# A two-layer hybrid trunk (gated linear attention beside chunked attention) in float32: softmax's negated maximum from one pass, a head's normaliser as one power, small sums off GpSimd, heads turned later, last chunks bank by bank

## The chip, the cores and the metric

The kernel runs on one core of one Trainium2 chip. A core has five engines that work side by side: TensorE (PE, matrix products, with its weight loads as PEld), VectorE (DVE), ScalarE (ACT), GpSimd (POOL) and SyncE (SP), which here only issues transfers. The metric is the device time of one execution in microseconds (us); lower is better. Each engine takes its instructions in the order in which they were placed in its stream and waits on semaphores for the others.

## The reference

Two layers, each on x of 512 tokens by 2048 features:

```python
h = rmsnorm(x, g_pre)
z = h @ w_in                                   # 7184 columns, split into nine parts
gq, gk, gv, gg, ga, aq, ak, av, ag = split_columns(z)
log_a = log_sigmoid(ga @ w_alpha + b_alpha) / GLA_TAU
o_gla = gla_chunk_causal(gq, gk, gv, log_a)     # 4 heads, state carried over 8 chunks of 64
o_gla = rmsnorm(o_gla, g_gla) * silu(gg)        # norm within a head
o_att = chunk_band_attention(aq, ak, av, rel_bias)   # 8 heads of 128
o_att = rmsnorm(o_att, g_att) * silu(ag)
y = concatenate([o_gla, o_att]) @ w_out
return x + rmsnorm(y, g_post)
```

In attention the scores are `q k^T * 128**-0.5 + bias`, a query sees all keys of its own and of earlier chunks, the softmax runs over the keys, and each head's output is divided by its root mean square (with EPS = 1e-6 under the root) before the gate.

## The kernel before

**Products in split precision.** Every float32 operand is split into a high and a low part (`wh` and `wl` for weights, made by ScalarE at L183 and VectorE at L187), and each product is three matrix products: high by high, high by low, low by high. The weights lie in 18 blocks of 512 columns per layer, and each block in eight chunks of 256 rows. A chunk of a block, or a Strassen-like sum of chunks of two blocks, is a *job*: `load` fetches it, `high` and `low` split it, `ahead()` prepares the next jobs. `std_gemm` does one block for up to four groups of 128 tokens, chunk by chunk (24 matrix products of 512 columns a chunk over four groups); `fast_gemm` does a pair of blocks in seven sums of products (P1, P5, P6, P3, P7, P2, P4), four jobs each, 28 jobs in all, 12 products of 512 columns or 24 of 256 a job. When a sum is complete, `consume` reads the accumulators: P3 and P7 give the two halves of the pair's second block, P2 and P4 those of its first.

**Order of the blocks in a layer.** AG0 and AG1 (gate of attention, `std_gemm`), then the pairs GG, AV, QK01 with QK23, QK45 with QK67, GK with GQ, GV0 with GV1 (`PAIRS`, `fast_gemm`), then the output projection: its first two blocks by `std_gemm` (NB_IN and NB_IN + 1), its last two as one pair with `end=True`.

**Side work.** All that is not a large product is written as generators in the list `tasks`. After each job, or each group of products of a chunk, `Pace` calls `pump(n)`, which takes n steps of the first task in the list, n being `rate` per call on average. `until(cond)` takes steps without any product between them until a condition holds; `drain()` empties the list. The side work is: `attend` for a pair of heads, in the step order of `ORDER` (S scores, T transposes of the probabilities, P the product with the values, G the gate, R the turn of the head's output into the layout of the output projection; 0 to 3 are groups of 128 tokens; "-" is an empty step); `forget_gate_decay`; `transpose_q`; and `gla_heads` for two GLA heads in four units of 256 tokens each (`new`, `states`, `read`, `norm`, `gate`, `turn`).

**Who waits for whom in the program.** Heads are taken in the order 2 and 3, 0 and 1, 6 and 7, 4 and 5. `heads_done` is set at the end of `attend`. The consumer of the fourth Q and K set waits for heads 2 and 3 (L829); the forget gate, put at the head of the list, for heads 0 and 1 (L847); the first consumed half of GK/GQ for heads 6 and 7 (L866), the first of GV for heads 4 and 5 (L1034). `operand_out` (L1048) waits until a GLA head's turned output is in `og`; the chunks of the output projection come in the order `OO`, with GLA heads 0 and 1 last.

**Buffers.** Four PSUM banks `mm` hold the accumulators, four `ax` everything else. Temporaries `t` rotate through eight buffers; the gate tile `sg` that a head (L751) or a GLA unit (L912) fetches has two, the bias tile two, small statistics `sm` six. `wh` has four buffers, `wl` three.

**The planner.** The kernel is written in a framework that places the semaphores and sets each engine's order with a planner (L1191): it runs through the program with its own estimates of costs and gives an engine, whenever it is free by these estimates, the first instruction of the program that is ready by them. A step's place in the program is so a priority, not a fixed place; what the planner has put in order stays so on the chip, however long things take there.

**The steps that the change touches.** Scores: L723 adds the bias to the scores in PSUM and gives the maximum; L727 negates it on GpSimd; L728 takes exp with that as bias and the row sum as second output; after the last group L731 and L732 invert the sums and scale them, and L733 asks for a later head's bias (L698, with a fill of one corner at L699). L762 squares the output, scaled by the inverted sum; `gate` (L764) makes the head's coefficient: EPS is added on GpSimd (L399), the power -0.5 taken there (L395), the result multiplied by the inverted sum (L767), and L770 gates the four groups. L781 turns the head on TensorE, L784 scales it, L787 and L793 store it. For GLA: L904 outer products, L922 and L924 states, L937 read, L947 squares, L399 and L395 the norm, L955 the gate, L965 the turn, L976 its scaling, L105 and L106 the split, L980 the store. Output projection: L1069 and L1070 empty a bank.

## Time and profile before

| | |
|---|---|
| median of three runs | 1717.86 us (1715.18 to 1718.84) |
| the profiled execution: its own time | 1714.22 us |
| its span from first to last instruction | 1712.5 us |
| TensorE busy | 1651.8 us, 96% of the span |
| VectorE, ScalarE, GpSimd busy | 1206.1, 870.3, 207.9 us |
| mean granted TensorE clock | 0.987 |

Times in views of the trace count from the first instruction of the profiled execution. A matrix product's row gives a modelled duration that overlaps its neighbours; how fast products follow each other is seen from their starts. "[2.8 <-DVE sg L770]" behind a row says that the engine was idle for 2.8 us before it and that the instruction at L770, VectorE's write of `sg`, released it. In the list of waits a row gives the us in total, how often, and the longest. "PEclk" is the clock that the chip granted TensorE, as a share of full speed.

### The profile page before, as it was taken

To read this page: it belongs to the slowest core of one execution; us is meant where nothing else is said; L and a number is where in the kernel's file an instruction comes from. 1 tells how busy PE (TensorE), PEld (TensorE's weight loads), DVE (VectorE), ACT (ScalarE), POOL (GpSimd) and SP (SyncE) were. 2 spreads that over 40 slices of the span, in tenths; PEclk is the share of its full clock that TensorE was granted. 3 is DMA by queue.
4 is the path that set the end of the run, shared out by engine and by line. 5 is a ranking of instruction groups with operands and counts; after the bars stand their busy time and mean duration, and the time that the engine had idled before them with its cause. 6 is when DMAs were issued, how large, how long until landed. Compare 5 with 4: busy or idle time off the path is not lost.

```text
span 1712.5 us, 25057 instructions
## 1 busy us (share of the span) xinstructions
PE 1651.8 (96%) x9090; PEld 1410.9 (82%) x9090; DVE 1206.1 (70%) x1547; ACT 870.3 (51%) x1444; POOL 207.9 (12%) x368
## 2 busy tenths in 40 slices
PE   7999999999999999899989999999999999998996
PEld 5888889999987877688778878799999878776784
DVE  5746867776866875468987567767778667753787
ACT  8634544465664644335694345445556555433443
POOL 0110000011201101210212000000111112012101
PEclk9999999999999999999999999999999999999998
DMA  7986886868857787489769687868686777865994
GB/s 254 361 308 236 324 289 237 290 194 284 299 172 262 241 330 247 164 308 326 263 228 386 222 304 282 303 226 284 209 305 235 235 239 245 315 218 178 348 331 145
DMA packets 143004, 455.05 MB, mean 266 GB/s; under 512 B 15444, under 2 KB 32212, under 8 KB 142880
## 3 DMA queue, kind: packets, MB, share of 16 engines
q1 hardware_dynamic: 119984, 373.76, 63.7%
q0 software_dynamic: 22176, 78.41, 11.9%
q8 instruction: 72, 1.18, 0.3%
q10 hardware_dynamic: 720, 1.28, 0.2%
q14 instruction: 52, 0.43, 0.1%
HBM read 381.28 MB, written 72.11 MB: 265 GB/s over the span
## 4 chain that ended last, share of the span: by engine, by line
PE 87%; DMA 4%; DVE 4%; issue 2%; ACT 2%; POOL 0%; SPq 0%; DVEq 0%; POOLq 0%; ACTq 0%
PE mm L349 41%; PE mm L339 18%; PE mm L275 18%; PE ax L756 2%; DMA raw<-in_w_dram 2%; DVE wl L187 1%; PE ax L904 1%; DMA sa<-S 1%; PE ax L739 1%; PE ax L937 1%; PE ax L597 1%; ACT wh L183 1%; PE ax L720 1%; PE ax L718 1%; PE ax L719 1%
## 5 line engine op out<-in xcount | busy, mean ns | idle before, releaser
L349 PE MATMUL mm<-wh,sa 128*128 128x512 f32 x1536 | 488.1, 393 | 2.8 <-DMA sa<-S 1.6
L183 ACT CAST wh<-raw 128x1024 fp32r<-128x1024 f32 x248 | 261.9, 1056 | 293.5 <-PE mm L349 96.9
L187 DVE TENSOR_TENSOR wl<-raw,wh 128x1024 fp32r<-128x1024 f32 x248 | 301.2, 1217 | 81.7 <-PE mm L275 26.3
L183 ACT CAST wh<-H 128x1024 fp32r<-128x1024 f32 x224 | 234.6, 1051 | 210.3 <-PE mm L349 112.4
L349 PEld LDWEIGHTS mm<-wh,sa 128*128 128x128 f32 x1536 | 288.1, 188 | 64.3 <-DMA sa<-S 2.5
L187 DVE TENSOR_TENSOR wl<-H,wh 128x1024 fp32r<-128x1024 f32 x224 | 272.6, 1221 | 93.2 <-PE mm L349 26.9
L349 PE MATMUL mm<-wl,sa 128*128 128x512 f32 x768 | 301.8, 393 | 7.6 <-DVE wl L187 7.5
L339 PE MATMUL mm<-sa,wh 128*128 128x256 f32 x1280 | 236.0, 285 | 0.0
L339 PEld LDWEIGHTS mm<-sa,wh 128*128 128x128 f32 x1280 | 200.2, 191 | 0.2
L349 PE MATMUL mm<-wh,a 128*128 128x512 f32 x576 | 186.3, 397 | 2.4 <-DVE g L1070 1.4
L275 PE MATMUL mm<-wh,a 128*128 128x512 f32 x512 | 171.3, 399 | 15.1 <-ACT a L105 7.8
L339 PE MATMUL mm<-sa,wl 128*128 128x256 f32 x640 | 182.1, 285 | 0.4 <-DVE wl L187 0.4
L349 PEld LDWEIGHTS mm<-wl,sa 128*128 128x128 f32 x768 | 144.5, 188 | 41.8 <-DVE wl L187 12.1
L176 DVE TENSOR_TENSOR H<-H,raw 128x1024 f32<-128x1024 f32 x112 | 136.5, 1219 | 2.0
L349 PEld LDWEIGHTS mm<-wh,a 128*128 128x128 f32 x576 | 109.8, 191 | 26.6 <-DVE g L1070 1.9
L275 PEld LDWEIGHTS mm<-wh,a 128*128 128x128 f32 x512 | 96.9, 190 | 38.9 <-ACT a L105 9.2
L180 DVE TENSOR_TENSOR raw<-H,raw 128x1024 f32<-128x1024 f32 x48 | 58.8, 1225 | 91.4 <-DMA raw<-in_w_dram 91.4
L339 PEld LDWEIGHTS mm<-sa,wl 128*128 128x128 f32 x640 | 122.5, 191 | 0.6 <-DVE wl L187 0.6
L349 PE MATMUL mm<-wl,a 128*128 128x512 f32 x288 | 114.4, 397 | 0.3 <-DVE wl L187 0.3
L275 PE MATMUL mm<-wl,a 128*128 128x512 f32 x256 | 102.4, 400 | 0.0
L727 POOL TENSOR_SCALAR sm<-sm 128x1 f32<-128x1 f32 x64 | 34.1, 533 | 521.7 <-DVE sm L723 520.9
L339 PE MATMUL mm<-a,wh 128*128 128x256 f32 x512 | 95.2, 286 | 0.0
(191 smaller groups left out, 2418.0 us busy)
## 6 DMA issues: line engine op xcount, KB each, us to landing
raw<-in_w_dram SPq DMA_DIRECT2D x312, 512.0 KB, 4.9
sa<-S SPq DMA_DIRECT2D x192, 512.0 KB, 4.7
H<-in_w_dram SPq DMA_DIRECT2D x56, 512.0 KB, 4.7
sa<-A SPq DMA_DIRECT2D x48, 512.0 KB, 5.8
S<-g POOLq DMA_DIRECT2D x32, 512.0 KB, 7.7
oS<-g POOLq DMA_DIRECT2D x32, 512.0 KB, 6.8
sa<-oS SPq DMA_DIRECT2D x32, 512.0 KB, 5.0
sg<-t POOLq DMA_DIRECT2D x32, 256.0 KB, 5.7
```

The costliest lines, as they stand in the source:

```text
L176: nc.vector.tensor_tensor(out=h, in0=h, in1=r, op=ALU.add)
L180: nc.vector.tensor_tensor(out=r, in0=h, in1=r, op=ALU.subtract)
L183: last_cast[0] = nc.scalar.copy(self.wh, src).ins
L187: nc.vector.tensor_tensor(out=self.wl, in0=self.src, in1=self.wh.bitcast(F32), op=ALU.subtract)
L275: nc.tensor.matmul(pss[o], a[:, part, t], rhs[:, kk, :], start=(i == 0 and kk == 0 and m == 0), stop=(i == n - 1 and kk == 1 and m == 2),)
L339: nc.tensor.matmul(dst, lhs[:, kk, f], a[:, part, tok], start=(fresh and kk == 0 and m == 0 and ft % 2 == 0), stop=(c == 3 and kk == 1 and ...
L349: nc.tensor.matmul(out_ps[t], a[:, part, tok], rhs[:, kk, :], start=(fresh and kk == 0 and m == 0), stop=(c == 3 and kk == 1 and m == 2), ...
L597: nc.tensor.matmul(ps[0:96, half * 256 : (half + 1) * 256], wga[kt // 10][:, kt % 10, :], op[:, i, (kt % 2) * 256 : (kt % 2 + 1) * 256], s ...
L718: nc.tensor.matmul(ps[:, :n], self.qh[:, t], self.kh[:, :n], start=True, stop=False)
L719: nc.tensor.matmul(ps[:, :n], self.qh[:, t], self.kl[:, :n], start=False, stop=False)
L727: nc.gpsimd.tensor_scalar(out=nmx, in0=mx, scalar1=-1.0, scalar2=None, op0=ALU.mult)
L756: nc.tensor.matmul(o, self.pt[i][:, j * P : (j + 1) * P], av[hd // 4, j // 2][:, j % 2, (hd % 4) * P : (hd % 4 + 1) * P], start=(j == 0), ...
```

## The change

It has six parts.

1. **Softmax.** The scaled queries are split with -128**-0.5, so the scores come out negated, and the bias tile is negated by a ScalarE copy after its transfer, before VectorE's fill. L723 adds and takes a *minimum*, which is the negated maximum; exp runs with scale -1 and that minimum as its bias. The GpSimd negation goes.
2. **A head's normaliser.** The square is scaled by a constant, not by the inverted sum. Instead of the inverted sums a tile `el` = EPS times the squared sums is made; the coefficient is (mean square + `el`) to the power -0.5: one addition on VectorE and one power on GpSimd.
3. **Small sums.** `rms_scale`, which GLA's norm uses, adds EPS on VectorE.
4. **Turns.** A list `delayed` holds turns with a count of pumped steps: a head's turn runs eight steps after its gate, a GLA unit's five steps after its gate. `heads_done` is set by the turn of the pair's second head. `ORDER` loses its two turns and its leading and trailing pauses and gets one pause before each gate; the first pair starts after five empty steps. `pump` counts a step also when only delayed turns are left. The forget gate and `gla_heads` get more empty steps, and the rates change: 2.1 for the last four pairs, 1.7 for the first output block.
5. **GLA's gate tile** lies in `sg` for odd units and in a buffer of the bias tile for even ones.
6. **Last chunks bank by bank.** AG1 and the second output block run with lag 2, the first output block with lag 1: the last `lag` chunks are done bank after bank, and each bank is emptied when it is complete.

```diff
--- before.py
+++ after.py
@@ -116,8 +116,8 @@
     ident = cst[:, 0:P]
     chunk_ind = cst[:, 2 * P : 2 * P + 2]
     ones = cst[:, 2 * P + 2 : 3 * P + 2]
+    mhalf = cpool.tile([P, 4], F32, tag="mhalf", name="mhalf")
     later = cpool.tile([P, P], F32R, tag="later", name="later")
-    mhalf = cpool.tile([P, 4], F32, tag="mhalf", name="mhalf")
 
     CO = (0, 4, 1, 5, 2, 6, 3, 7)
     OO = (5, 4, 7, 6, 2, 3, 0, 1)
@@ -225,22 +225,30 @@
             prepare(what, i + n)
 
     tasks = []
+    delayed = []
 
     def pump(n):
-        while n > 0 and tasks:
-            try:
-                next(tasks[0])
-                n -= 1
-            except StopIteration:
-                tasks.pop(0)
+        while n > 0 and (tasks or delayed):
+            for entry in list(delayed):
+                entry[0] -= 1
+                if entry[0] <= 0:
+                    delayed.remove(entry)
+                    entry[1]()
+            while tasks:
+                try:
+                    next(tasks[0])
+                    break
+                except StopIteration:
+                    tasks.pop(0)
+            n -= 1
 
     def until(cond):
         while not cond():
-            assert tasks
+            assert tasks or delayed
             pump(1)
 
     def drain():
-        while tasks:
+        while tasks or delayed:
             pump(1)
 
     class Pace:
@@ -396,7 +404,7 @@
 
     def rms_scale(out_r, ms):
         v = sm(ms.shape[-1])
-        nc.gpsimd.tensor_scalar(out=v, in0=ms, scalar1=EPS, scalar2=None, op0=ALU.add)
+        nc.vector.tensor_scalar(out=v, in0=ms, scalar1=EPS, scalar2=None, op0=ALU.add)
         rsqrt(out_r, v)
 
     def square_sum(out_ss, pieces):
@@ -534,8 +542,8 @@
     ps_w = aux()
     for i in range(10):
         nc.tensor.matmul(ps_w, warm[:, 0:P], warm, start=True, stop=True)
+    nc.gpsimd.memset(mhalf, -0.5)
     nc.vector.tensor_copy(later, cst[:, P : 2 * P])
-    nc.gpsimd.memset(mhalf, -0.5)
 
     fg_weights = {}
 
@@ -645,11 +653,13 @@
                 lah, lal = t2(dtype=F32R), t2(dtype=F32R)
                 split(lah, lal, la)
                 yield
+                yield
                 pend.append((t, la, lah, lal))
                 if t:
                     finish_tile(*pend.pop(0))
                     yield
-            yield
+            for _ in range(4):
+                yield
             finish_tile(*pend.pop(0))
             yield
             nc.scalar.activation(a_end, ps_end[:, 0:32], AF.Exp)
@@ -668,7 +678,7 @@
         tasks.append(token_sums(l))
         tasks.append(forget_gate())
         std_gemm(l, AG0, (2, 3), CO, operand_in, gate_evac(1, 0), rate=0.8)
-        std_gemm(l, AG1, range(NT), CO, operand_in, gate_evac(1, 1), rate=1.3)
+        std_gemm(l, AG1, range(NT), CO, operand_in, gate_evac(1, 1), rate=1.3, lag=2)
         drain()
         fast_gemm(l, PAIRS[0], gate_consume)
         act_table("natural_log_exp_and_others")
@@ -696,7 +706,8 @@
             b = tmp.tile([P, 512], F32, tag="bias", name=nm("bias"), bufs=2)
             src = rel[l, HEADS[n]]
             nc.sync.dma_start(b, bass.AP(tensor=src.tensor, offset=src.offset + 127, ap=[[639, P], [1, 512]]))
-            nc.vector.memset(b[0:64, 448:512], NEG)
+            nc.scalar.activation(b, b, AF.Copy, scale=-1.0)
+            nc.vector.memset(b[0:64, 448:512], -NEG)
             biases[HEADS[n]] = b
 
         heads_done = set()
@@ -719,17 +730,17 @@
                 nc.tensor.matmul(ps[:, :n], self.qh[:, t], self.kl[:, :n], start=False, stop=False)
                 nc.tensor.matmul(ps[:, :n], self.ql[:, t], self.kh[:, :n], start=False, stop=True)
                 pr = self.prob[i] = t2((lk,))
-                mx, nmx = sm(1), sm(1)
+                nmx = sm(1)
                 nc.vector.tensor_tensor_reduce(
-                    out=pr, in0=ps[:, :lk], in1=biases[self.hd][:, 512 - lk : 512], op0=ALU.add, op1=ALU.max,
-                    scale=1.0, scalar=NEG, accum_out=mx,
+                    out=pr, in0=ps[:, :lk], in1=biases[self.hd][:, 512 - lk : 512], op0=ALU.add, op1=ALU.min,
+                    scale=1.0, scalar=-NEG, accum_out=nmx,
                 )
-                nc.gpsimd.tensor_scalar(out=nmx, in0=mx, scalar1=-1.0, scalar2=None, op0=ALU.mult)
-                nc.scalar.activation(pr, pr, AF.Exp, bias=nmx, accum_out=self.lsum[:, i : i + 1])
+                nc.scalar.activation(pr, pr, AF.Exp, bias=nmx, scale=-1.0, accum_out=self.lsum[:, i : i + 1])
                 if i == 0:
-                    self.rl, self.rs = sm(4), sm(4)
-                    nc.vector.reciprocal(self.rl, self.lsum)
-                    nc.gpsimd.tensor_scalar(out=self.rs, in0=self.rl, scalar1=P ** -0.5, scalar2=None, op0=ALU.mult)
+                    self.el = sm(4)
+                    nc.vector.scalar_tensor_tensor(
+                        out=self.el, in0=self.lsum, scalar=EPS, in1=self.lsum, op0=ALU.mult, op1=ALU.mult
+                    )
                     load_bias(HEADS.index(self.hd) + 2)
 
             def trans(self, i):
@@ -759,12 +770,12 @@
                         start=(j == 0), stop=(j == i),
                     )
                 jk = t2((P,), BF16)
-                nc.scalar.activation(jk, o, AF.Square, scale=self.rs[:, i : i + 1], accum_out=self.ss[:, i : i + 1])
+                nc.scalar.activation(jk, o, AF.Square, scale=P ** -0.5, accum_out=self.ss[:, i : i + 1])
 
             def gate(self):
-                r, cf = sm(4), sm(4)
-                rms_scale(r, self.ss)
-                nc.vector.tensor_tensor(out=cf, in0=r, in1=self.rl, op=ALU.mult)
+                v, cf = sm(4), sm(4)
+                nc.vector.tensor_tensor(out=v, in0=self.ss, in1=self.el, op=ALU.add)
+                rsqrt(cf, v)
                 for i in range(NT):
                     dst = self.sg[:, i, :]
                     nc.vector.scalar_tensor_tensor(
@@ -793,12 +804,20 @@
                         nc.gpsimd.dma_start(oa_d[l][half, c], flat(z))
 
         ORDER = (
-            "- - aS3 aS2 aS1 aS0 aT3 bS3 aT2 aP3 bS2 aT1 aP2 bS1 aT0 aP1 bS0 aP0 aG "
-            "bT3 bT2 bP3 bT1 bP2 aR bT0 bP1 bP0 bG - - - - bR"
+            "aS3 aS2 aS1 aS0 aT3 bS3 aT2 aP3 bS2 aT1 aP2 bS1 aT0 aP1 bS0 aP0 - aG "
+            "bT3 bT2 bP3 bT1 bP2 bT0 bP1 bP0 - bG"
         ).split()
 
         def attend(hd, qk):
             heads = {"a": Head(hd, qk, 0), "b": Head(hd + 1, qk, 1)}
+
+            def turn(h):
+                h.turn()
+                if h.hd % 2:
+                    heads_done.add(hd)
+
+            for _ in range(5 if hd == HEADS[0] else 0):
+                yield
             for step in ORDER:
                 if step == "-":
                     yield
@@ -810,12 +829,10 @@
                     h.trans(int(step[2]))
                 elif step[1] == "P":
                     h.mix(int(step[2]))
-                elif step[1] == "G":
+                else:
                     h.gate()
-                else:
-                    h.turn()
+                    delayed.append([8, lambda h=h: turn(h)])
                 yield
-            heads_done.add(hd)
 
         QKT = {(0, 1): ("g4", "g5", "g6", "g7"), (0, 0): ("g8", "g9", "g10", "g11"),
                (1, 1): ("g12", "g13", "g14", "g15"), (1, 0): ("g4", "g5", "g6", "g7")}
@@ -832,7 +849,7 @@
                 hs = slice(h * 256, (h + 1) * 256)
                 hi, lo = sets[j][2 * b][:, :, hs], sets[j][2 * b + 1][:, :, hs]
                 if b == 0:
-                    split_scaled(hi, lo, z, QS)
+                    split_scaled(hi, lo, z, -QS)
                 else:
                     split(hi, lo, z)
                 if h and b:
@@ -841,8 +858,8 @@
 
         load_bias(0)
         load_bias(1)
-        fast_gemm(l, PAIRS[2], qk_consume(0), rate=2, feature_major=True)
-        fast_gemm(l, PAIRS[3], qk_consume(1), rate=2, feature_major=True)
+        fast_gemm(l, PAIRS[2], qk_consume(0), rate=2.1, feature_major=True)
+        fast_gemm(l, PAIRS[3], qk_consume(1), rate=2.1, feature_major=True)
 
         until(lambda: 0 in heads_done)
         tasks.insert(0, forget_gate_decay())
@@ -876,7 +893,7 @@
             nc.vector.tensor_tensor(out=z, in0=kd, in1=decay[h][:, t, :], op=ALU.mult)
             split(kdh[h][:, t, :], kdl[h][:, t, :], z)
 
-        fast_gemm(l, PAIRS[4], kq_consume, rate=2)
+        fast_gemm(l, PAIRS[4], kq_consume, rate=2.1)
 
         gla_done = set()
         og = {}
@@ -908,7 +925,8 @@
 
             def states(self):
                 h, p = self.h, self.p
-                self.sg = sgt([2, 256])
+                tag = "sg" if (2 * h + p) % 2 else "bias"
+                self.sg = tmp.tile([P, 2, 256], F32, tag=tag, name=nm(tag), bufs=2)
                 nc.sync.dma_start(
                     self.sg,
                     sg_d[l][0][p * 256 : (p + 1) * 256, h * 256 : (h + 1) * 256].rearrange("(t p) c -> p t c", p=P),
@@ -989,28 +1007,28 @@
                 units.append(Unit(h, p, gvh, gvl, units[-1] if p else None))
                 units[-1].outer()
 
+            for _ in range(4):
+                yield
             new(0)
             yield
             units[0].states()
             yield
-            for k in range(5):
+            for k in range(4):
                 if k < 3:
                     new(k + 1)
                     yield
-                if k < 4:
-                    units[k].read()
-                    yield
+                yield
+                units[k].read()
+                yield
                 if k < 3:
                     units[k + 1].states()
                     yield
-                if k:
-                    units[k - 1].turn()
-                    yield
-                if k < 4:
-                    units[k].norm()
-                    yield
-                    units[k].gate()
-                    yield
+                units[k].norm()
+                yield
+                yield
+                units[k].gate()
+                delayed.append([5, units[k].turn])
+                yield
             gla_done.update((2 * j, 2 * j + 1))
 
         gvh, gvl = {}, {}
@@ -1106,12 +1124,12 @@
                     yield from load_forget_gate(l + 1)
 
         x_src = x if l == 0 else x_mid
-        std_gemm(l, NB_IN, range(NT), OO, operand_out, out_evac(0), rate=1.8)
+        std_gemm(l, NB_IN, range(NT), OO, operand_out, out_evac(0), rate=1.7, lag=1)
         until(lambda: len(og) == 8)
         tasks.append(output_sums(l))
         xs0 = load_tokens(0, x_src, nc.gpsimd)
         xs1 = load_tokens(1, x_src, nc.gpsimd)
-        std_gemm(l, NB_IN + 1, range(NT), OO, operand_out, out_evac(1), rate=0.8)
+        std_gemm(l, NB_IN + 1, range(NT), OO, operand_out, out_evac(1), rate=0.8, lag=2)
         drain()
         gains = [load_gain(2 + j) for j in range(2)]
         for c in range(4):
```

## The prediction

> **What bounds the kernel now.** I read the page first.
>
> ```profile
> span 1712.5 us, 25057 instructions
> ...
> PE 1651.8 (96%) x9090; PEld 1410.9 (82%) x9090; DVE 1206.1 (70%) x1547; ACT 870.3 (51%) x1444; POOL 207.9 (12%) x368
> ```
>
> TensorE is the bound. The change takes no matrix product away, so it can win only where TensorE stands still or runs at a lower clock. The second view is therefore the list of what TensorE waited for over the whole span (total us, times, longest us).
>
> ```profile
> PE mm L349 <- DVE wl L187: 7.8, 11, 2.6
> PE mm L275 <- ACT a L105: 7.8, 4, 2.7
> PE ax L458 <- DVE g L448: 7.4, 2, 7.2
> PE ax L781 <- DVE sg L770: 5.6, 2, 2.8
> PE mm L275 <- DVE g L1070: 4.5, 2, 2.2
> ...
> PE mm L349 <- DVE g L1070: 1.4, 1, 1.4
> ...
> PE ax L756 <- ACT wh L183: 0.5, 1, 0.5
> PE mm L339 <- DVE wl L187: 0.4, 1, 0.4
> ```
>
> L458 is the start of the kernel and L187 the splitting of weights: the change leaves both alone. L781 is a head's turn; the longest waits of the first L275 row, 2.7 us, and all of the first L1070 row belong to the output projection; the last two rows are all that attention stops TensorE for in its own stage. So the change has two places to earn in: the end of the third head pair, and the end of the output projection's first block, in each layer. I asked for the stretch around each (length, PE busy, PEld, DVE, ACT, POOL, granted clock, DMA share, GB/s).
>
> ```profile
> 525.00:545.00 20.00, 16.04 (x69) 12.76 (x68) 9.97 (x17) 7.01 (x15) 3.66 (x6) 0.83 0.89 324
> 700.00:735.00 35.00, 30.09 (x145) 23.03 (x144) 12.85 (x21) 13.40 (x34) 8.50 (x15) 0.95 0.56 188
> 1365.00:1385.00 20.00, 16.02 (x69) 12.84 (x68) 11.65 (x19) 7.86 (x19) 3.69 (x6) 0.83 0.88 312
> 1545.00:1575.00 30.00, 25.09 (x114) 19.04 (x113) 11.44 (x19) 10.36 (x27) 8.19 (x15) 0.94 0.65 217
> ```
>
> In the first and third stretch TensorE is idle for 20.00 - 16.04 = 3.96 and 3.98 us, and the clock of 0.83 costs 20 x 0.17 = 3.4 us more: 7.4 us each. In the other two it is idle for 4.91 us, and the clock costs 35 x 0.05 and 30 x 0.06 = 1.8 us: 6.7 us each. Together 28.2 us, the most that the two places can give.
>
> **The change part by part.** *The head's turn.* The order of time at 533 us (start, length, idle before and its releaser):
>
> ```profile
> 533.47 0.49 PE L756 MATMUL ax<-g,t 128*128 128x128 f32 x2 [1.05 <-ACT t L762]
> ...
> 533.99 0.37 ACT L762 ACTIVATE t<-ax,sm 128x128 bf16<-128x128 f32 x1 [0.58 <-PE ax L756]
> ...
> 534.55 0.27 POOL L399 TENSOR_SCALAR sm<-sm 128x4 f32<-128x4 f32 x1 [4.92 <-ACT t L762]
> ...
> 534.90 1.04 POOL L395 TENSOR_TENSOR sm<-sm,mhalf 128x4 f32<-128x4 f32 x1
> 535.98 0.16 DVE L767 TENSOR_TENSOR sm<-sm,sm 128x4 f32<-128x4 f32 x1 [1.25 <-POOL sm L395]
> 536.25 1.13 DVE L770 SCALAR_TENSOR_TENSOR sg<-ax,sm,sg 128x128 f32<-128x128 f32 x4
> ...
> 536.75 1.16 PE L781 MATMUL ax<-cst,sg 128*128 128x128 f32 x4 [2.79 <-DVE sg L770]
> 537.29 1.28 DVE L311 TENSOR_TENSOR t<-mm,ev 128x512 f32<-128x512 f32 x2
> ```
>
> This is the burst at line 866: the first product that closes in the GK/GQ pair may not be consumed before heads 6 and 7 are done. Counting the steps that the pace gives: 18 in the QK23 half, 56 in the next pair, 30 up to the sixteenth job of GK/GQ, 15 of them spent on the forget gate, leave 21 of that task's 34 steps done; 13 run in one go, the four pauses before the last turn pass at once, and only after the turn may L311 free the accumulator for which the next matrix products wait. By the new numbers (39 of 58 steps are gone when the first task starts, so 19; then 58; then 31, less 22 for a forget gate with seven more pauses; tasks of 33, 28, 28 and 28 steps) 25 of 28 steps are done. Three are left, and the turn then stands eight steps behind the gate: seven of them are steps of heads 4 and 5 that give TensorE 15 score products and 7 transposes. Of the products one row tells the price:
>
> ```profile
> L718 PE MATMUL ax<-g,g 128*128 128x512 f32 (+1 forms) x64 | 21.9, 352 | 0.0
> ```
>
> 15 x 0.35 = 5.3 us of work in a wait that was 2.79 us. The gate's chain itself gets shorter: L399 (0.27 us) leaves GpSimd, for an addition on VectorE as long as L767 (0.16). What is late next is L311, some 7 us after the burst begins; it has the four jobs of P7 as cover, four times 12 products. I leave 1.0 us of the 7.4, what L756 waited for L762 (1.05); bounds are none left and all left. **Gain 2 x 6.4 = 12.8 us.** The turn brings its GpSimd stores (L787, L793) and, through the sg buffer that it frees, SyncE's fetch at L751 along; the next fetch that needs that buffer is ten steps behind the turn, so weight loads behind it on SyncE should not stand.
>
> *The GLA units.* TensorE at the end of the first output block:
>
> ```profile
> 716.81 0.60 PE L965 MATMUL ax<-cst,sg 128*128 128x128 f32 x4
> 720.08 0.79 PE L275 MATMUL mm<-wh,a 128*128 128x512 f32 x1 [2.67 <-ACT a L105]
> ...
> 724.30 0.60 PE L965 MATMUL ax<-cst,sg 128*128 128x128 f32 x4
> 727.13 0.50 PE L275 MATMUL mm<-wh,a 128*128 128x512 f32 x1 [2.23 <-DVE g L1070]
> ```
>
> The block is 32 groups of six products; a product takes 21.77 / 96 = 0.227 us where nothing disturbs it, a group 1.36:
>
> ```profile
> 98.81 21.77 PE mm L275 x96
> ```
>
> By steps, the last two turns were due after groups 15 and 17 (18 + 1.8 per group, steps 45 and 48). They ran after 28 and 30 (twelve products stand between them, and twelve behind the last), 13 groups late. What held them was, by the trace, the gate tile's two buffers: a fetch is issued right after a turn, each time.
>
> ```profile
> 683.64 0.60 PE L965 MATMUL ax<-cst,sg 128*128 128x128 f32 x4
> ...
> 684.44 0.40 SPq L912 DMA_DIRECT2D sg<-sg  x1
> ...
> 700.20 0.60 PE L965 MATMUL ax<-cst,sg 128*128 128x128 f32 x4
> ...
> 700.83 0.38 SPq L912 DMA_DIRECT2D sg<-sg  x1
> ```
>
> The change puts every other unit's tile into the bias buffers, four in all, and that hold falls. But it also begins four steps later, adds pauses and lowers the pace to 1.7: by steps (19 + 1.7 per group, steps 64 and 69) the last two turns are now due after groups 27 and 30, which is where they stood anyway. The first gains one group of cover: 2.67 - 1.36 = 1.3 us of stop left; the second is used by the very next group: 2.2 left. With half of the clock's 1.8, 4.4 of 6.7 us remain. **Gain 2 x 2.3 = 4.6 us**; bounds: all 6.7 gained, or 13 groups of 1.36 lost (below).
>
> On that clock: a stop of 2.83 us left the granted clock at 1.00 in one stretch, a stop of 2.04 us was followed by 0.83 in another.
>
> ```profile
> 864.35 0.73 PE L275 MATMUL mm<-wh,a 128*128 128x512 f32 x2 [2.83 <-DVE a L106]
> ```
>
> ```profile
> 857.00:867.00 10.00, 7.13 (x32) 5.07 (x30) 9.30 (x18) 9.97 (x27) 1.94 (x5) 1.00 0.65 229
> 885.00:895.00 10.00, 7.96 (x35) 6.27 (x33) 6.07 (x10) 8.81 (x18) 2.16 (x4) 0.83 0.65 235
> ```
>
> Hence the half. The Trainium skill ("TensorE: Matmul & The Clock Gate", Part 1) lets the clock fall only after an idle window of about 3.4 us; by that rule neither remaining stop would cost clock and the sum would be 1.8 us lower, but the 0.83 after a 2.04 us stop speaks against it.
>
> *Last chunks bank by bank.* Lag 1 gives the first output block the same order as lag 0. Lag 2 in the second block empties banks up to 8 us before the next pair needs them: the 1.4 us of "L349 <- DVE g L1070", which stands once, goes. **Gain 1.4 us.** In AG1 no wait of this kind has a row: nothing. The price of lag 2 is that two jobs hold their weights for all eight groups; the three wl buffers still let the split of the following job end about when TensorE reaches it: nothing, with L187's 2.6 us twice as the bound.
>
> *Softmax.* The hop over GpSimd goes, with its reciprocal's product:
>
> ```profile
> L727 POOL TENSOR_SCALAR sm<-sm 128x1 f32<-128x1 f32 x64 | 34.1, 533 | 521.7 <-DVE sm L723 520.9 <-DVE bias L699 0.8
> L728 ACT ACTIVATE t<-t,sm 128x512 f32<-128x512 f32 (+1 forms) x64 | 35.9, 561 | 73.9 <-POOL sm L727 73.9
> ```
>
> The rest of this part (the sums of four columns that go to VectorE, the square's fixed scale, the earlier fill of `mhalf`) costs or gives fractions of a us on engines that are not the bound, beside TensorE's products. ScalarE's 73.9 us of idling is not TensorE's: attention stops TensorE for 0.5 + 0.4 us. **Gain 0.5 us**, bounds 0 and 0.9.
>
> *The negated bias* is an added ScalarE copy, 16 times 128x512, 0.64 us each by this row, 10 us on an engine that is half idle:
>
> ```profile
> L105 ACT CAST g<-g 128x512 fp32r<-128x512 f32 x32 | 20.4, 643 | 17.4 <-DMA S<-g 16.8 <-DVE g L503 0.6
> ```
>
> It waits for the bias's transfer, where only VectorE's fill did, and the fill now waits for the copy. At the start of layer 1 that wait reached TensorE:
>
> ```profile
> 888.12 0.11 DVE L699 MEMSET bias<- 64x64 f32 x1 [5.17 <-DMA bias<-in_rel_dram]
> ...
> 888.86 0.73 PE L275 MATMUL mm<-wh,g 128*128 128x512 f32 x2 [2.04 <-DVE g L106]
> ```
>
> Behind the copy on ScalarE stand weight casts and splits. One copy's length longer costs 0.6 us; if the planner puts both instructions later, 2.04 + 1.7 of clock are gained; if ScalarE stands for the whole 5.17 beside VectorE, 3.1 are lost. **Loss 0.6 us.** The same page of the Trainium skill (section "Architectural detail: the array is 16× 32×32, not 1× 128×128") calls ScalarE and VectorE strictly first in, first out; by it all behind the copy stands, which is the 3.1.
>
> The sum: 12.8 + 4.6 + 1.4 + 0.5 - 0.6 = 18.7 us off the profiled execution's own 1714.2, 1695.5. The median of the runs, 1717.9, lies 3.6 above that execution, so **1699.2 us**, 1.1% faster. Its own range is 1690 to 1708.
>
> **Rivals.** *All of GLA's stop goes too* (the turns run earlier than due, or TensorE fills with the next block): 2 x 4.4 less, 1690.4. For it: the buffers were what held; against it: the steps.
>
> *The head's stop only moves*, as the delayed turn is still the last thing before L311: the 12.8 are not gained, 1712.0. For it: L311 still stands behind a turn; against it: 5.3 us of products where there were none.
>
> *Slower: the units stay as late against their steps as they were.* If not the buffers but the chain of norm, gate and turn made the 13 groups, the last turn comes 13 x 1.36 = 17.7 us after TensorE has nothing else to do, in each layer: 1699.2 + 35.4 = 1734.6. It passes 1717.9 from 7 groups on (1699.2 + 2 x 7 x 1.36 = 1718.2). For it: turns came 7.5 us (716.81 to 724.30) to 8.3 us (two from 700.20) apart at the end, which no step asks for; against it: the fetch behind each turn.
>
> *The change does nothing here*: the planner orders by readiness and moves work past the pauses: 1717.
>
> **How the numbers follow.** 0.52 for the forecast, 0.14 for all of GLA, 0.12 for the moved stop, 0.08 for nothing, 0.14 for slower. Two tenths of a per cent (3.4 us) is about what a measurement of this kernel can tell from no change. Faster is the first two and most of the third, 0.76; same is the fourth and the third's rest, 0.10; slower 0.14. The range reaches from 1684 (all of GLA, the bias's 3.7 and 0.6, and the 2.0 that I leave at the heads' turns) to 1716 (the moved stop with the bias's loss, and GLA units up to 6 groups late); outside lie the slower case and half of nothing.
>
> **What would show it.** At the end of the third head pair no wait of L781 on L770, and a clock of 1.00; in its place score products (L718 to L720). L965 before the end of the first output block with a fetch no longer tied to it, and a first wait on L105 of about 1.3 us. No L727, and Exp released by VectorE. The bias copy's wait on ScalarE at layer 1's start under 5 us. The forecast is wrong if the last L965 comes more than 7 groups after TensorE has run out, or if the 3.4 us of lost clock at the third pair stay.

## The result, and the profile after

The changed kernel takes **1702.08 us** (1700.32 to 1704.39, four runs), the kernel before, run beside it, 1718.33 us (1715.18 to 1718.84). The ratio is **0.991** (95% interval 0.9892 to 0.9928): about 0.9% faster. A second measurement, in the third group of experiments below, gave 0.9912 (0.9891 to 0.9933).

The page of the changed kernel; its profiled execution took 1702.84 us, that of before 1714.22.

```profile
span 1701.1 us, 24915 instructions
...
PE 1648.9 (97%) x9090; PEld 1403.5 (83%) x9090; DVE 1209.9 (71%) x1563; ACT 873.2 (51%) x1460; POOL 160.0 (9%) x256
```

TensorE has the same 9090 products; the span is 11.4 us shorter. What TensorE waited for (us in total, times, longest):

```profile
PE mm L357 <- DVE wl L187: 10.4, 13, 2.6
...
PE mm L357 <- DVE t L319: 2.6, 2, 1.3
PE mm L283 <- DVE g L1088: 1.9, 4, 0.6
PE mm L283 <- ACT a L105: 1.8, 1, 1.8
PE ax L767 <- DVE sm L734: 1.1, 2, 0.6
```

The head's turn (L792, before L781) no longer waits for its gate. The waits of an output product (L283, before L275) on L105 fell from four to one, those on L1088 (before L1070) from at most 2.2 us to at most 0.6. New are two waits of 1.3 us on L319 (before L311), the combination that empties the banks of the GK/GQ pair. The stretches of the prediction again, in the same columns (length, PE, PEld, DVE, ACT, POOL, granted clock, DMA share, GB/s):

```profile
525.00:545.00 20.00, 17.66 (x90) 14.46 (x89) 14.30 (x30) 10.76 (x25) 3.30 (x5) 1.00 0.90 307
700.00:735.00 35.00, 33.72 (x165) 25.72 (x162) 15.86 (x28) 12.09 (x30) 7.68 (x13) 1.00 0.69 227
1365.00:1385.00 20.00, 18.03 (x99) 15.12 (x98) 12.53 (x28) 9.65 (x25) 2.70 (x4) 1.00 0.87 312
1545.00:1575.00 30.00, 28.72 (x132) 22.25 (x131) 13.36 (x21) 12.29 (x30) 6.37 (x11) 1.00 0.71 242
```

The clock is 1.00 in all four. TensorE stands 2.34 and 1.97 us at the end of the third head pair (before 7.4 each with the clock), and 1.28 and 1.28 us at the end of the first output block (before 6.7 each). That is 28.2 - 6.9 = 21.3 us gained in the two places, more than the 11.4 us by which the profiled spans differ. The order of time at the third pair (start, length, what it waited for) shows what is left; in this and the later excerpts rows between those shown are left out:

```profile
537.48 0.66 PE L792 MATMUL ax<-cst,sg 128*128 128x128 f32 x4 [0.47 <-ACT t L753]
538.69 1.16 PE L767 MATMUL ax<-g,t 128*128 128x128 f32 x8 [0.55 <-DVE sm L734]
...
540.43 1.28 DVE L319 TENSOR_TENSOR t<-mm,ev 128x512 f32<-128x512 f32 x2
...
541.17 0.50 PE L357 MATMUL mm<-wh,a 128*128 128x512 f32 x1 [1.32 <-DVE t L319]
```

0.47 + 0.55 + 1.32 = 2.34: L319 is still behind the turn. At the end of the first output block:

```profile
710.47 0.38 ACT L965 ACTIVATE t<-ax 128x256 bf16<-128x256 f32 x1 [1.67 <-PE ax L955]
711.38 0.60 PE L983 MATMUL ax<-cst,bias 128*128 128x128 f32 x4
712.62 0.88 DVE L973 SCALAR_TENSOR_TENSOR sg<-ax,sm,sg 128x256 f32<-128x256 f32 x2 [1.11 <-POOL sm L403]
714.58 0.60 PE L983 MATMUL ax<-cst,sg 128*128 128x128 f32 x4
715.50 0.72 PE L283 MATMUL mm<-wh,a 128*128 128x512 f32 x2 [0.33 <-DVE a L106]
718.20 0.50 PE L283 MATMUL mm<-wh,a 128*128 128x512 f32 x1 [0.58 <-DVE g L1088]
719.10 0.62 ACT L105 CAST g<-t 128x512 fp32r<-128x512 f32 x1
724.00 0.39 PE L283 MATMUL mm<-wh,g 128*128 128x512 f32 x1
```

The last unit's norm (L965 at 710.47) now comes ahead of the turn of the unit before it (L983 at 711.38), its gate (L973) at 712.62, and the last two turns are 3.2 us apart, where they were 7.5. From 715.50 to 718.2 TensorE works off the last chunk's first half; from 718.20 on it waits for no turn: L1088 has emptied a bank, and the products up to 724.00 can only be the next block's, for the operand of the last turn, `g`, is split from 719.10 on and is first used at 724.00. TensorE passes the time with the next block.

To see where the rest went I counted, from one product's start to the next, what goes beyond the usual distance of products of that shape, and summed it by stage, both layers together (us; "else" is all other stages):

| kernel | GK/GQ pair | next pair | first output block | else | sum |
|---|---|---|---|---|---|
| before | 19.0 | 12.5 | 22.1 | 55.1 | 108.7 |
| changed | 10.2 | 13.2 | 11.8 | 62.0 | 97.2 |
| changed, measured again | 10.3 | 10.3 | 11.6 | 58.3 | 90.5 |

The first output block gains 10.3, the GK/GQ pair 8.8. The sums fall by 11.5 and 18.2, as the profiled spans do (11.4, and 18.1 in the execution measured again). The two executions of the same changed kernel differ by 6.7 us in sum, spread over stages that wait for weights and transfers; "else" is between 49 and 62 over all the kernels below. Below some 7 us only single stages of this table can be compared, not its sums. One shift in "else" is easy to name, at the passage from layer 0 to layer 1:

```profile
830.69 0.80 PE L357 MATMUL mm<-wl,sa 128*128 128x512 f32 x1 [2.56 <-DVE wl L187]
...
881.15 0.33 PE L466 MATMUL ax<-cst,g 128*128 128x128 f32 x1 [1.82 <-ACT g L476]
```

These two stops have taken the place of the 2.83 and 2.04 us that stood at 864 and 888 us before.

### The profile page after: what moved, and what is told of

It is laid out like the page before. It is cut to its first block, busy times and chain, and to the rows that moved or that the text cites. A ratio compares the mean times of both kernels' runs of the same rounds, so it can differ in the third digit from the quotient of the medians.

```text
span 1701.1 us, 24915 instructions
## 1 busy us (share of the span) xinstructions
PE 1648.9 (97%) x9090; PEld 1403.5 (83%) x9090; DVE 1209.9 (71%) x1563; ACT 873.2 (51%) x1460; POOL 160.0 (9%) x256
## 3 DMA queue, kind: packets, MB, share of 16 engines
q10 hardware_dynamic: 720, 1.28, 0.2%
## 5 line engine op out<-in xcount | busy, mean ns | idle before, releaser
L357 PE MATMUL mm<-wh,sa 128*128 128x512 f32 x1536 | 490.3, 394 | 9.1 <-ACT wh L183 4.0
L357 PEld LDWEIGHTS mm<-wh,sa 128*128 128x128 f32 x1536 | 289.7, 189 | 74.5 <-ACT wh L183 5.8
L357 PE MATMUL mm<-wl,sa 128*128 128x512 f32 x768 | 303.2, 395 | 9.5 <-DVE wl L187 9.4
L357 PE MATMUL mm<-wh,a 128*128 128x512 f32 x576 | 184.0, 393 | 2.6 <-DVE t L319 2.6
L357 PEld LDWEIGHTS mm<-wl,sa 128*128 128x128 f32 x768 | 145.4, 189 | 43.5 <-DVE wl L187 14.5
L283 PE MATMUL mm<-wh,a 128*128 128x512 f32 x512 | 169.4, 395 | 3.6 <-ACT a L105 1.8
L357 PEld LDWEIGHTS mm<-wh,a 128*128 128x128 f32 x576 | 107.3, 188 | 25.1 <-DVE t L319 3.0
L403 POOL TENSOR_TENSOR sm<-sm,mhalf 128x2 f32<-128x2 f32 (+2 forms) x44 | 53.2, 1210 | 688.6 <-DVE sm L777 459.9
L283 PEld LDWEIGHTS mm<-wh,a 128*128 128x128 f32 x512 | 95.9, 188 | 26.0 <-ACT a L105 2.3
L357 PE MATMUL mm<-wl,a 128*128 128x512 f32 x288 | 113.5, 394 | 0.9 <-DVE wl L187 0.9
L283 PE MATMUL mm<-wl,a 128*128 128x512 f32 x256 | 100.5, 393 | 0.5 <-DVE wl L187 0.4
L347 PE MATMUL mm<-a,wh 128*128 128x256 f32 x512 | 94.8, 284 | 0.0
```

The source lines that it names most:

```text
L283: nc.tensor.matmul(pss[o], a[:, part, t], rhs[:, kk, :], start=(i == 0 and kk == 0 and m == 0), stop=(i == n - 1 and kk == 1 and m == 2),)
L347: nc.tensor.matmul(dst, lhs[:, kk, f], a[:, part, tok], start=(fresh and kk == 0 and m == 0 and ft % 2 == 0), stop=(c == 3 and kk == 1 and ...
L357: nc.tensor.matmul(out_ps[t], a[:, part, tok], rhs[:, kk, :], start=(fresh and kk == 0 and m == 0), stop=(c == 3 and kk == 1 and m == 2), ...
L403: nc.gpsimd.tensor_tensor(out=out_r, in0=v, in1=mhalf[:, : v.shape[-1]], op=ALU.pow)
```

## The experiments

All of them compute the same function. Those named u are the changed kernel with one part undone, a the kernel before with one part done, g and v change something new. Three groups of four ran, each on one chip with its own runs of the kernel before (medians 1713.66, 1712.58 and 1714.23 us); ratios are against those. The changed kernel itself ran in the third group alone, so in the first two ratio is set against ratio.

My theory was the prediction's: the heads' turns are worth most, through the delay of eight steps; the GLA turns were late because of two gate tiles; softmax is worth nothing.

### u1: softmax and normaliser as before

```diff
-            nc.scalar.activation(b, b, AF.Copy, scale=-1.0)
-            nc.vector.memset(b[0:64, 448:512], -NEG)
+            nc.vector.memset(b[0:64, 448:512], NEG)
...
-                nmx = sm(1)
+                mx, nmx = sm(1), sm(1)
...
+                nc.gpsimd.tensor_scalar(out=nmx, in0=mx, scalar1=-1.0, scalar2=None, op0=ALU.mult)
-                nc.scalar.activation(pr, pr, AF.Exp, bias=nmx, scale=-1.0, accum_out=self.lsum[:, i : i + 1])
+                nc.scalar.activation(pr, pr, AF.Exp, bias=nmx, accum_out=self.lsum[:, i : i + 1])
...
```

The maximum, its negation on GpSimd, the inverted sums and the positive query scale are those of before.

> The changed kernel with the softmax and the normaliser of before: maximum, negation on GpSimd, inverted sums; no copy of the bias on ScalarE. Theory: attention stopped TensorE for 0.9 us in all, so the time stays within 3 us of the changed kernel's 1702 (0.989 to 0.993). Rival (fewer small tiles and a shorter way from scores to exp let the planner place attention better): 5 us or more are lost, 1707 and up (0.994 and up).

Measured: 1698.37 us, 0.9904 (0.9887 to 0.9921), no slower than the changed kernel. In the changed kernel Exp is indeed released by VectorE (total idle time before the 64 and what ended it):

```profile
L738 ACT ACTIVATE t<-t,sm 128x512 f32<-128x512 f32 (+1 forms) x64 | 35.8, 559 | 30.3 <-DVE sm L734 26.7 <-ACT t L753 1.6 <-ACT t L773 1.0
```

ScalarE's idle time there fell from 73.9 to 30.3 us, and the time of the kernel has nothing of it. In one place TensorE does stand longer without this part: in u1 20.00 - 17.21 = 2.79 and 20.00 - 15.97 = 4.03 us after the third head pair (525 to 545 and 1365 to 1385 us), against 2.34 and 1.97 in the changed kernel, the first at a clock of 0.91. As in u2 below, the time does not show it.

### u2: heads turned in the gate's own step

```diff
-                    delayed.append([8, lambda h=h: turn(h)])
+                    turn(h)
```

> The changed kernel, with each head turned in the step of its gate instead of eight steps later. Theory (the late turn is what removes the stop at the end of the third head pair): the wait of the turn on the gate comes back in the GK/GQ pair, with its 3.4 us of half clock, and the time rises by 5 us per layer, 10 in all, to about 1712 us (0.996 of the kernel before). Rival (the stop went because the gate's chain became shorter and the pauses went, not because of the delay): less than 3 us, 1702 to 1705 (0.991 to 0.993).

Measured: 1697.95 us, 0.9906 (0.9889 to 0.9922). The stop came back in its place:

```profile
525.00:545.00 20.00, 16.10 (x65) 12.60 (x64) 9.69 (x17) 6.00 (x12) 2.70 (x4) 0.83 0.79 294
```

```profile
533.29 1.20 PE L792 MATMUL ax<-cst,sg 128*128 128x128 f32 x4 [2.64 <-issue]
534.53 0.69 ACT L795 ACTIVATE t<-ax,gcol 128x512 f32<-128x512 f32 x1 [2.80 <-PE ax L792]
535.01 1.28 DVE L319 TENSOR_TENSOR t<-mm,ev 128x512 f32<-128x512 f32 x2
535.75 0.79 PE L357 MATMUL mm<-wh,a 128*128 128x512 f32 x1 [1.26 <-DVE t L319]
```

yet the time did not. ("issue" says that the profile names nothing that the turn waited for; the gate before it, L781, started at 532.84. In layer 1 the stop is 3.8 us.) By stage: 19.9 us in the GK/GQ pair against 10.2 and 10.3, but 6.4 in the pair after it against 13.2 and 10.3. Together the two pairs lose 26.3, against 23.4 and 20.6 in the changed kernel: 3 to 6 us of difference by stage, which the times (0.9906 against 0.991 and 0.9912, each to some 0.2%) neither show nor exclude. The 10 us of my theory fell. What keeps u2's two pairs 5 us below the kernel before (26.3 against 31.5), the new `ORDER`, the rate of 2.1 or the shorter chain of the gate, no run separates.

### u3: GLA's gate tile in `sg` alone

```diff
-                tag = "sg" if (2 * h + p) % 2 else "bias"
+                tag = "sg"
```

> The changed kernel with GLA's gate tile in its two old buffers alone. Theory (the two buffers held the turns 13 groups behind their steps): the last two turns again wait for one another through the fetch, the stop at the end of the first output block returns, 4 to 5 us per layer, 1711 us (0.996). Rival (the order of the steps and the pauses did it): within 3 us of 1702.

Measured: 1698.44 us, 0.9907 (0.9891 to 0.9924), and 11.6 us lost in the first output block as with four tiles. Its last two turns, both out of `sg`:

```profile
711.92 0.60 PE L983 MATMUL ax<-cst,sg 128*128 128x128 f32 x4
715.13 0.60 PE L983 MATMUL ax<-cst,sg 128*128 128x128 f32 x4
```

3.2 us apart again. The two buffers did not hold the turns. Counted in groups of six products from the block's first, the last two turns of u3 come after 26.7 and 28.7, as in the changed kernel.

### u4: GLA's old order

```diff
-            for _ in range(4):
-                yield
...
-                delayed.append([5, units[k].turn])
...
+                if k:
+                    units[k - 1].turn()
+                    yield
+                if k < 4:
+                    units[k].norm()
...
```

The whole loop of before is back, without the new pauses, with rate 1.8; lag 1 and the four tiles stay.

> The changed kernel with the order of GLA's steps from before (turn of the unit before in line, no pauses, no delay, 1.8 steps per group), but four gate tiles and the sum on VectorE. Theory (buffers): the stop at the end of the first output block stays as small as in the changed kernel, within 3 us of 1702. Rival (order, pauses and delay): the stop of 2.7 and 2.2 us with its clock loss returns, 1711 us (0.996).

Measured: 1708.69 us, 0.9959 (0.9944 to 0.9975); against 0.9904 to 0.9907 of its three neighbours on the same chip that is 9 us. The waits are those of before:

```profile
PE mm L283 <- ACT a L105: 7.9, 4, 2.7
...
PE mm L283 <- DVE g L1088: 4.5, 2, 2.2
```

and the order of time shows how they come about:

```profile
714.70 0.60 PE L983 MATMUL ax<-cst,bias 128*128 128x128 f32 x4
715.85 0.83 ACT L994 ACTIVATE t<-ax,gcol 128x256 f32<-128x256 f32 x2
716.57 0.38 ACT L965 ACTIVATE t<-ax 128x256 bf16<-128x256 f32 x1
717.97 0.50 PE L283 MATMUL mm<-wh,a 128*128 128x512 f32 x1 [2.67 <-ACT a L105]
718.56 0.87 DVE L973 SCALAR_TENSOR_TENSOR sg<-ax,sm,sg 128x256 f32<-128x256 f32 x2
722.28 0.74 PE L983 MATMUL ax<-cst,sg 128*128 128x128 f32 x4
725.25 0.50 PE L283 MATMUL mm<-wh,a 128*128 128x512 f32 x1 [2.23 <-DVE g L1088]
```

The turn of the last unit but one (714.70) is called out by the product that needs it (717.97). Only behind its copy (L994) follows the last unit's norm (L965, 716.57), then its gate (718.56) and its turn (722.28), called out in turn two groups later. Both turns stand after 28 and 30 groups, as in the kernel before, although there are four tiles. (u4's profiled execution is the longest of its twelve, 1713.83 us, so its stops are at the upper end.)

### a3: GLA's new order alone, on the kernel before

The edit of u4 the other way round, with the new `pump` and rate 1.7.

> The kernel before with the new step order, pauses and 5-group turn of the gated linear attention alone (and the first output block's rate 1.7). Theory (this order is what earns, and it needs nothing else of the change): the stops of 2.7 and 2.2 us at the end of the first output block go in both layers, the block falls from 65.5 to about 62.7 us, with the clock 10 us in all, ratio 0.993 to 0.995; the 6.4 us after the third pair stay. Rival (the order pays only with the rest of the change, the heads' turns or the lag above all): less than 4 us, ratio 0.998 or more.

Measured: 1708.55 us, 0.9974 (0.996 to 0.9988): 4.4 us, between theory and rival. Its first output block loses 14.2 us instead of 22.1, so 7.9 of the 10.3 need nothing else of the change.

### g1: the old GLA order, with the last norm first

Against u4:

```diff
+                if k == 3:
+                    units[k].norm()
+                    yield
                 if k:
                     units[k - 1].turn()
                     yield
-                if k < 4:
+                if k < 3:
                     units[k].norm()
```

> The changed kernel with the old order of the gated linear attention (which alone gave 0.9959), but the last unit's norm put ahead of the turn of the unit before it. Theory (what earned is only that the last unit's norm and gate are done before the turn that the output block waits for, so that the last turn follows 3 us behind and not 7.6): both stops of the block go, 62.7 us for it, ratio 0.990 to 0.992. Rival (what earned is that the whole chain is spread by the pauses and turned with a delay): the wait of 2.7 us on the turn's operand stays, ratio 0.995 to 0.997.

Measured: 1696.46 us, 0.9899 (0.9878 to 0.9921) (u4 0.9959): 0.6% for one step that changed places with its neighbour. The stretch and its last turns:

```profile
700.00:735.00 35.00, 35.00 (x165) 28.50 (x164) 17.92 (x26) 16.06 (x35) 7.15 (x13) 1.00 0.79 259
```

```profile
712.16 0.49 PE L983 MATMUL ax<-cst,bias 128*128 128x128 f32 x3
712.48 0.60 PE L983 MATMUL ax<-cst,sg 128*128 128x128 f32 x4
```

TensorE is not idle for a moment, and the last two turns stand back to back. The first output block falls from u4's 67.3 to 59.5 us in each layer, while the pair before it keeps its length (95.0 and 95.0 us; in layer 1 94.8 and 94.6; lengths from a stage's first product to the next stage's first). The two kernels ran on different chips, each against its own runs of the kernel before, and the intervals of the ratios lie apart. Pauses, delay and lower rate are not what earns; the place of the last unit's norm is.

### u5: without the two lags of 2

```diff
-gate_evac(1, 1), rate=1.3, lag=2)
+gate_evac(1, 1), rate=1.3)
-out_evac(1), rate=0.8, lag=2)
+out_evac(1), rate=0.8)
```

> The changed kernel without the two lags of 2 (second gate block, second output block). Theory (the 4 to 5 us that the products of the last pair of the output blocks lose in layer 0, against the kernel before, come from elsewhere, and the lag is worth under 2 us): ratio 0.990 to 0.993, the stop of 1.5 us at the end of the second output block of layer 1 is back. Rival (banks freed one after the other is what shifts the steps and costs those 4 to 5 us): ratio 0.988 or less. Second rival (the lag is a main earner): 0.994 or more.

Measured: 1698.58 us, 0.9914 (0.9896 to 0.9932): as the changed kernel. The second output block loses 1.7 us in both layers together, against 1.2 with the lag: of the stop of 1.5 us in layer 1 that I expected back only some 0.5 us is there. Nor is the lag needed for the rest: in a3, which has no lag, the second output block takes 44.2 us in each layer as in the changed kernel (before: 43.5 and 45.1). The last pair of layer 0 and the start of layer 1 lose 11.3 us, against 13.7 and 12.1 with it and 10.7 before: where the 4 to 5 us of the last pair in layer 0 come from stays open; 2 to 4 of them are given back at the start of layer 1.

### v1: the query halves settled before the wait for the heads

The burst of the prediction (line 866 of before) has an order of its own: `kq_consume` first waits until heads 6 and 7 are turned, and then settles the half that is ready, which empties its banks by L319. v1 settles both halves first; the first half's transposes then come with the second's. (The halves are those of GQ, the pair's second block, so queries; the expectation calls them key halves.)

```diff
-                if not gqT:
-                    until(lambda: 6 in heads_done)
-                    gqT.extend(slot(tag, [2, 512]) for tag in ("g12", "g13"))
-                tasks.insert(0, transpose_q(2 * h + t, settled(src, comb)))
+                z = settled(src, comb)
+                if t:
+                    if not gqT:
+                        until(lambda: 6 in heads_done)
+                        gqT.extend(slot(tag, [2, 512]) for tag in ("g12", "g13"))
+                    for i, w in enumerate((first_z.pop(h), z)):
+                        tasks.insert(0, transpose_q(2 * h + i, w))
+                else:
+                    first_z[h] = z
```

> The changed kernel, with the two key halves of the fifth pair settled (combined out of the banks) before the wait for the sixth head's turn, not behind it. Theory (the combination that the tensor engine waits 1.3 us for in each layer stands behind the turn's copies only because of that order): the two waits of 1.3 us go, with the products behind them running on, 2 to 3 us, ratio 0.989 to 0.990. Rival (the next thing in line, the split or the key slots freed by the turn, takes its place): same as the changed kernel, 0.990 to 0.992, with the wait under another name.

Measured: 1689.24 us, 0.9857 (0.9835 to 0.9879), some 9 us better than the changed kernel, more than either theory said: not only the two waits of 1.3 us went, but all that was left in the place:

```profile
525.00:545.00 20.00, 20.00 (x107) 17.02 (x106) 15.47 (x32) 13.07 (x29) 2.70 (x4) 1.00 0.93 318
...
1360.00:1380.00 20.00, 20.00 (x111) 17.13 (x110) 13.48 (x32) 13.27 (x32) 2.70 (x4) 1.00 0.88 313
```

The GK/GQ pair loses 4.6 us instead of 10.2, the next pair 9.2 instead of 13.2 or 10.3. The banks are now emptied long before they are needed:

```profile
523.90 1.28 DVE L319 TENSOR_TENSOR t<-mm,ev 128x512 f32<-128x512 f32 x2
...
533.31 0.39 PE L357 MATMUL mm<-wh,a 128*128 128x512 f32 x1
```

The product at 533.31 is the first of P2, which needs the banks of P3; products of P7 read `sa`, those of P2 `a`. Between P3 and P2 stand the 48 products of P7, 48 x 0.227 = 10.9 us of work. In v1 L319 comes 3.1 us after the first product of P7 (520.80), and P2 does not wait. In the changed kernel it comes 17.9 us after it (522.53 to 540.43), in the kernel before 18.8 (L311, 518.51 to 537.29), and the first product of P2 follows it at 541.17 and 538.02: P7 was used up, and for 6.4 us no product of the pair started.

### v3: v1, with the heads turned at once

The edits of v1 and of u2 together.

> The changed kernel with the key halves settled ahead of the wait for the sixth head's turn (which alone gave 0.9857), and the heads turned in the gate's own step again. Theory (the late turn is worth its 4 us in each layer only where nothing else stands behind the turn, so that the gain hidden before now counts): the stop of 3.8 us in front of the head's transposes is back in both layers, 8 us with the clock, ratio 0.990 to 0.992. Rival (the late turn is worth nothing, whatever else is done; the products behind make it up again): 0.985 to 0.987.

Measured: **1686.11 us, 0.9836** (0.9815 to 0.9858), a little below the rival's 0.985 to 0.987 and the lowest median of all. It answers what u2 left open:

```profile
525.00:545.00 20.00, 20.00 (x100) 16.93 (x99) 15.52 (x28) 10.86 (x22) 2.70 (x4) 1.00 0.86 298
...
1360.00:1380.00 20.00, 19.80 (x102) 16.31 (x101) 13.96 (x26) 10.94 (x25) 2.70 (x4) 1.00 0.89 324
```

```profile
533.46 1.03 POOL L403 TENSOR_TENSOR sm<-sm,mhalf 128x4 f32<-128x4 f32 x1 [25.13 <-DVE sm L777]
534.53 1.13 DVE L781 SCALAR_TENSOR_TENSOR sg<-ax,sm,sg 128x128 f32<-128x128 f32 x4 [1.16 <-POOL sm L403]
534.55 0.61 PE L357 MATMUL mm<-wh,a 128*128 128x512 f32 x2
535.70 0.49 PE L792 MATMUL ax<-cst,sg 128*128 128x128 f32 x3
```

The chain of power, gate and turn is the one that stopped TensorE in u2, step for step, right behind the gate. But TensorE goes on with products of the pair (L357), because their banks have been emptied, and the turn waits for nobody. By v1 and v3, what stopped TensorE in the changed kernel and in u2 was not that the turn came late or early, but that the emptying of the banks stood behind it. The trace of the kernel before shows the same order (the gate at 536.25, L311 at 537.29); v1's edit on that kernel alone was not run.

### a1: the heads' turns put off, on the kernel before

The new `pump`, `ORDER`, first five steps and the delay of 8, without the rates of 2.1.

> The kernel before with the heads' turns put off by 8 steps and the new order of their steps alone (rates as before). Theory (the local stop goes and half of it is given back in the next pair, as in the changed kernel against the one with the heads turned at once): the stop of 6.4 us after the third pair goes, the pair after it loses some of it, ratio 0.996 to 1.000. Rival, from the prediction (12.8 us of heads' turns): 0.992 to 0.993.

Measured: 1706.37 us, 0.9952 (0.9934 to 0.9969): 7.9 us, between the two. The GK/GQ pair loses 17.0 us instead of 19.0, the next pair 8.1 instead of 12.5. Here the score products and their transposes themselves stop TensorE; whether the lower rate or the old softmax, which a1 also has, makes it, no run shows:

```profile
525.00:545.00 20.00, 17.57 (x80) 14.45 (x79) 14.66 (x30) 10.53 (x27) 6.32 (x13) 0.83 0.79 275
```

```profile
535.18 0.39 PE L726 MATMUL ax<-g,g 128*128 128x256 f32 x1 [1.53 <-DVE sm L731]
...
536.37 1.12 PE L747 MATMUL ax<-cst,t 128*128 128x128 f32 x4 [0.56 <-ACT t L736]
...
537.83 0.79 PE L726 MATMUL ax<-g,g 128*128 128x512 f32 x1 [0.35 <-DVE sm L731]
```

### v2: v1 and g1 together, and the changed kernel again

> The changed kernel with two things: the key halves settled ahead of the wait for the sixth head's turn (0.9857 alone) and the old order of the gated linear attention with the last unit's norm first (0.9899 alone, against 0.991 for the changed kernel). Theory (they act at different places, the first in the fifth and sixth pair, the second in the first output block, which is 3.2 us shorter in a layer, of which the sixth pair before it takes back 5 in the one and 2 in the other): 0.984 to 0.986. Rival (the sixth pair now bears more steps of the attention and loses what the first won): 0.987 to 0.990.

> The changed kernel itself once more, beside the three others on one chip: 0.989 to 0.993 (0.9892 to 0.9928 was measured). All theories alike; it says how far this chip is comparable with the ones before.

v2 measured 1688.09 us, 0.9841 (0.9819 to 0.9864): as expected, and not told apart from v1 or v3; the next pair loses 11.4 us, where v1 has 9.2 and v3 6.2, so what the first output block gains (9.8 for 11.6) is given back in the pair ahead of it. The changed kernel again gave 1699.88 us, 0.9912 (0.9891 to 0.9933), as in the first measurement. v3 against it on the same chip is 13.8 us better.

## Why the prediction was right, and where not

The time was right (1699.2 forecast, 1702.1 measured; 18.7 us of gain forecast, 16.2 and 14.4 measured), and so were the bound, the two places and the sign. The two large terms of the sum were not: one was too large, the other too small, and that the sum came out close is in part luck.

*Heads' turns, 12.8 us forecast.* The signs came as described: no wait of the turn on its gate, clock 1.00, 2.34 us left, of which 1.32 on L319. In the place itself it was 5.1 and 5.4 us, 10.5; with the pair after it by stage 8.1 (first execution) or 10.9 (second); alone on the kernel before 7.9 (5.3 to 11.3 by the interval). So the term was over-sized by a few us: I left 1.0 us a layer and 2.34 and 1.97 were left. The larger error is the cause. I named the delay and its cover of score products; taking the delay back (u2) cost 3 to 6 us by stage and nothing that the times show. The step that failed is "What is late next is L311 ... it has the four jobs of P7 as cover". P7 is 10.9 us of work, L311 starts 18.8 us after P7's first product, and the next job's products wait for it: the cover was used up in the kernel before already, and in the changed kernel still is (17.9 us). L311 was not what is late next but the thing itself, as v1 and v3 show. My rival "the head's stop only moves" did not happen here, but its reason, L311 behind a turn, is the one that mattered.

*GLA units, 4.6 us forecast.* 6.7 - 1.28 = 5.4 us came off in each layer, 10.8 by the stretches and 10.3 by stage. In time it is 4.4 us when done alone (a3) and 9 when undone alone (u4); the intervals of the two (2.1 to 6.9 and, from those of u4 and its neighbours, some 5 to 13) overlap a little, and a3's block keeps 2.4 us more. Two steps failed. "What held them was, by the trace, the gate tile's two buffers": u3 has two buffers and loses nothing, u4 has four and its turns come after 28 and 30 groups as before; the fetch behind each turn that I took for the cause followed from the turn, it did not hold it. And "the second is used by the very next group: 2.2 left": TensorE took groups of the next block first, and 0.58 was left; of the first stop 0.33 (715.50), not 1.3. That was the mechanism of my first rival ("TensorE fills with the next block"), right in this place, while its total (1690.4) was not: the heads' term gave less, and in the first execution the other stages lost 6.9 us more than before ("else"). The slower rival, that norm, gate and turn themselves make the lateness, was right on the cause and wrong on the sign: the chain is the cause, but the change takes the last norm out from behind the turn before, and that was worth all of the stop (g1).

*Lag, 1.4 us.* By stage 1.4 fell to 1.2 in the second output block; u5 shows no difference in time. The stop went in layer 1 and a loss of 0.6 us came in layer 0, which I had not counted; u5 and a3, without the lags of 2, have it too, so it does not come from them.

*Softmax, 0.5 us, and the negated bias, -0.6.* u1 leaves both out and is the same within 0.2%. The bias copy at the start of layer 1 did not make the 2.04 us stop longer, as I had it; that stop is gone and others of the same size stand elsewhere. The copy (L709) runs at 887.30 us and ScalarE does not wait before it: the planner has put it later, one of the cases of the prediction, and the 3.1 us of the worst case were not lost. The Trainium skill ("TensorE: Matmul & The Clock Gate", section "Architectural detail: the array is 16× 32×32, not 1× 128×128") says that ScalarE keeps strict order; as the copy did not wait, this trace does not test that.

*Clock.* I left half of its cost in the output block, in case a stop above 2 us stayed. None stayed, and neither did the loss.

What I could not size beforehand is the rest of the kernel: the same program's stages that wait for weights and transfers differ by several us between two executions. 21.3 us were gained in the two places, 11.4 (first) and 18.1 (second) in the profiled span, 14 to 16 in the medians.

## What to carry to other kernels

When an engine waits behind a chain, ask first what the wait holds up, not how the chain could come earlier: here the heads could be turned at once when the banks were emptied ahead of it, and this earned some 9 us (v1), the change's own delay nothing that the times show (u2). In a pipeline of units written out by steps, the end counts: the last unit's norm must not stand behind the turn of the unit before it. A transfer that always follows an event shows that it depends on the event, not that the event waited for it.

## What the runs showed of the hardware

The granted clock does not go by the length of a single stop. In a1 it was 1.00 from 530 to 536 us, 0.50 from 536.2 to 542.8 and 1.00 from 543 to 548, so that the 0.83 over 20 us is an average of full and half; it fell after stops of 1.53 and 0.56 us, and the one of 0.35 us lies in the slow time already. In the changed kernel 0.47, 0.55 and 1.32 us, as close together, left it at 1.00. After a stop of 1.82 us that ended at 881.15 us, in the changed kernel, it was 0.50 from 881.8 to 885.0, an average of 0.83 here too (length, busy times, clock, DMA share, GB/s):

```profile
878.00:888.00 10.00, 8.10 (x45) 6.94 (x44) 4.69 (x7) 10.00 (x24) 1.67 (x3) 0.83 0.71 237
```

In the kernel before, the stop of 2.67 us that ended at 720.08 came with 0.50 from 719.7 to 722.9, while the next, of 2.23 us, was followed by no fall, nor was the one of 2.83 us at 864 us. 20 x 0.17 is 3.4 us: in a1 stops of 2.4 us in all came with a loss of clock of 3.4 us, more than the stops themselves. What decides, these runs do not show. The Trainium skill ("TensorE: Matmul & The Clock Gate", Part 1) calls the window in which the clock is decided free-running, about 3.4 us long; that it runs free would explain why the place of a stop counts, but an idle window of that length was not needed in these runs.
